# Strassen product (2,2) ahead of (5,1) in three feed-forward phases, with tiles 2 and 3 transposed half a product later, one copy in two halves, a bank of its own for a third row, and one evacuation moved to VectorE

## The chip, the cores and the metric

One core of a Trainium2 chip runs the kernel. The metric is device time in microseconds (us); the time given for a kernel is the median of several runs. The core has engines with a queue each, which take their instructions strictly in order: TensorE (PE) multiplies and transposes, VectorE (DVE) and ScalarE (ACT) work elementwise, GpSimd (POOL) and SyncE (SP) here mostly issue transfers. Engines wait for each other through semaphores. PE writes to eight banks of 128 x 512 floats; the operands come from on-chip memory, which the transfers fill.

## The reference, cut to what matters

The input is 512 positions of 1024 channels in float32. Two layers run, each as feed-forward, mixer, feed-forward, with a layer norm behind every one:

```python
def swiglu(x, w_gu, w_down):
    g, u = jnp.split(x @ w_gu, 2, axis=-1)
    return (jax.nn.silu(g) * u) @ w_down
...
for i in range(DEPTH):                      # DEPTH = 2
    x = layer_norm(ALPHA * x + 0.5 * swiglu(x, w_gu[i, 0], w_down[i, 0]), ln_g[i, 0], ln_b[i, 0])
    y = moba_attention(...) if i == 0 else pool_mixer(...)
    x = layer_norm(ALPHA * x + y, ln_g[i, 1], ln_b[i, 1])
    x = layer_norm(ALPHA * x + 0.5 * swiglu(x, w_gu[i, 1], w_down[i, 1]), ln_g[i, 2], ln_b[i, 2])
```

The width of the feed-forward is 2816. The order of the six phases, numbered n = 0 to 5, is: feed-forward, attention, feed-forward, feed-forward, pooling mixer, feed-forward.

## The kernel before, in words

**Matrix products.** The multiplications of the feed-forwards are done by Strassen's scheme: instead of eight products of quarter matrices there are seven (phase 0 takes one group in eight). A product (i, jj) is number i of group jj; a group makes 512 features of the gate and the up projection. Product 1 takes the first quarters, 2 the second, 5, 6 and 7 take sums and differences of quarters, 3 and 4 the rest. Every float32 operand is split into a rounded part `hi` and the remainder `lo`, and three matmuls (L110 to L112: lo x, hi x, hi x) stand for one. So a product is 24 matmuls of 128 x 512, and a "half product" (`q` 0 and 1 in `products`) 12. Each half takes one weight pair (`hi`, `lo`).

**What sets the order.** PE's order is that of the program (the engine is scheduled by hand); `order(eight)` lists the products of a feed-forward. The other engines' instructions are put in order by a scheduler, ahead of the run, which looks at when operands should be ready; each engine then keeps that fixed order. Tile pools give out buffers in turn, and a buffer's next writer waits for its last reader.

**Weights.** `pieces` is the list of loads, in order; `load` puts a piece of 512 KB on SP's queue (L302) and, where a sum of two quarters is wanted, has POOL's queue add the second in a transfer that accumulates (L304). `Quad` holds the pieces of one group: `p11`, `p12`, `s1` (a21 plus a22, an accumulation), `s3`, `p22`. With `apart` (groups 1 and 2 of phases 2, 3 and 5) DVE adds `s1` to `p11` for product 6 and `p11` to `p12` for product 3, at L158. `units` lists the weights in the order of use; `prepare` splits each into `hi` (ACT, L105) and `lo` (DVE, L106); the "lean" weights of the first products get their `lo` from ACT and an accumulating transfer on POOL's queue instead (L338). `p.uses` counts how many units still need a piece before its buffer may be loaded over.

**Start of a feed-forward.** The phase before ends with the normalisation of four tiles of 128 positions (`normalize`, L529 to L545: aggregate, variance, square root on ACT, reciprocal, one correction step, then the tile's two halves). `to_feature_major` transposes a normalised tile on PE (L487, eight transposes of 128 x 128), and ACT (L495) or DVE (L493) evacuates it into `st`, four pieces per half; the set `VEC` names the halves that DVE takes: tile 3, half 1. Tiles 0 and 1 are transposed inside the last products of the phase before. The transposes of tiles 2 and 3 are kept back in `late`, and `head` calls them after the two halves of product (1,1). From `st` the operands `x_1`, `x_2`, `x_3`, `x_5`, `x_6`, `x_7`, `x_4` are formed on DVE (differences, L429) and split (L105, L106).

**Behind a product.** `keep` copies the accumulator of products 1, 5 and 6 to on-chip memory (ACT, L735, one copy of 128 x 1024); products 2, 3, 4 and 7 finish a block: DVE adds the kept part (L745), ACT takes silu of one half (L727), DVE multiplies it by the other (L728), giving `gated`. Finished blocks wait in a list, and `to_features`, after products 5 and 4, transposes each on PE (L758, four transposes into one bank) and ACT copies it to `hT` (L759). The banks for it take turns: `TURNED` + 0 or 1, banks 6 and 7. With three blocks in the list the third uses the bank of the first again. `sums_at` gives the bank pair of product 1, 0 or 4; products 2 and 5 begin in pair `SECOND`, banks 2 and 3.

**Order around the change.** In phases 2, 3 and 5 the products start (1,1), (2,1), (1,2), (5,1), (6,1), (7,1), (3,1), (4,1) and go on with group 2: (2,2), (6,2), (5,2), and so on. (1,2) and (2,2) belong to group 2, whose weights are `w_gq[l, m, 2]` and `w_gq[l, m, 3]`, five quarters each.

Of the kernel before, what the change touches and what calls it, by code (L numbers as in the profile page):

```python
# [27 lines left out]
AF = mybir.ActivationFunctionType  # L28
# [34 lines left out]
VEC = ((3, 1),)  # L63
# [20 lines left out]
def trunk(ctx, tc, x_in, xt, rel_bias, ln_g, ln_b, w_gu, w_gq, w_dq, w_dh, w_v, a_in, a_out, b_in, b_group, b_scale, b_out, onehot, out):  # L84
    nc = tc.nc
# [11 lines left out]
    def bank(i, name):  # L97
        return banks8[:, i]

    def bank_pair(i):  # L100
        return banks8[:, i:i + 2]
# [20 lines left out]
    pieces, units, loaded, behind = [], [], [], {}  # L122

    def plain(src, lean=False):
        p = Piece(src)
        units.append((lambda: p.tile, (p,), src if lean else None))
# [51 lines left out]


    def order(eight):  # L180
        o = [(1, 1), (2, 1)] + ([(6, 1), (5, 1)] if eight else [(1, 2), (5, 1), (6, 1)])
        o += [(7, 1), (3, 1)] + [(1, 2)] * eight + [(4, 1)]
        steps = STEPS[not eight]
        for jj, following in zip(steps[1:], steps[2:] + (None,)):
            seven = [(i, jj) for i in (2, 6, 5, 7, 3, 4)]
            after = [(1, following)] if following is not None else []
            if jj == MIDDLE:
                group = [(i, FF) for i in LATER]
                o += seven[:-1] + group[:1] + seven[-1:] + group[1:] + after
            else:  # L190
                o += seven[:-1] + after + seven[-1:]
        return o + [(i, FF + 1) for i in DEEP]

    ORDERS = [order(True), order(False)]

    class Deep:
# [20 lines left out]
            units.append((lambda: p.tile, (p,)))  # L217

    BY_TRANSFER = ((1, 1), (2, 1), (1, 2))

    def in_turn(quads, kinds):
        pieces[-5 * len(quads):] = [q.pieces[k] for k in kinds for q in quads]
        return quads
# [14 lines left out]
    def two_quads(w, i):  # L238
        return in_turn([Quad(w[i + q]) for q in range(2)], (0, 2, 1, 3, 4))

    def ffn_units(l, m):
        eight = (l, m) == (0, 0)
        if eight:
            for i in FIRST:
                plain(w_gu[l, m, i])
        made = {}
        for i, jj in ORDERS[not eight]:
            lean = not eight and (i, jj) in BY_TRANSFER
            if (i, jj) == (1, 2) and not eight:
                for q in range(2):  # L250
                    plain(w_gq[l, m, 2 + q, 0], lean)
                b1 = pieces[-12:]
                pieces[-12:] = b1[0:2] + b1[4:6] + b1[2:4] + b1[10:] + b1[6:10]
                continue
            if jj not in made:
                if jj == 0:
                    made[jj] = [Quad(w_gu[l, m])]
                    pieces[-5:] = [made[jj][0].pieces[k] for k in (0, 2, 1, 3, 4)]
                elif jj == FF:
                    made[jj] = in_turn([Quad(w_dq[l, m, 0]), Quad(w_dq[l, m, 1]), narrow(Quad(w_dh[l, m]))], (0, 2, 1, 3, 4))  # L260
                elif jj == FF + 1:
                    made[jj] = in_turn([Deep(w_dq[l, m, q]) for q in (2, 3, 4)], range(5))
                else:
                    made[jj] = two_quads(w_gq[l, m], 2 * (jj - 1))
                for q in made[jj]:
                    if not eight and jj in (1, 2):
                        q.apart()
                    if i == 2:
                        q.p11.uses -= 1
            for q in made[jj]:  # L270
                q.unit(i, lean)

# [83 lines left out]
    def weights():  # L356
        taken[0] += 1
        while len(parts) < taken[0]:
            load_needed()
            prepare()  # L360
        return parts[taken[0] - 1]
# [7 lines left out]
    ax = glob.tile([P, NT, D], F32, name="ax")  # L369
# [110 lines left out]
            half, h = {1: (0, 0), 2: (1, 0), 3: (1, 1)}[i]  # L480
            return self.at(4 * half + k, (2 * h + t) * P, (2 * h + t + 1) * P)

    def to_feature_major(dest, t, half, xn, n, b):

        tp = bank(b + half, f"tp{t}_{half}")
        for i in range(4):
            nc.tensor.transpose(tp[:, i * P:(i + 1) * P], xn[:, (4 * half + i) * P:(4 * half + i + 1) * P], ident)  # L487
        src = dest.stage(half, t // 2)[:, :, (t % 2) * P:(t % 2 + 1) * P]
        for i in range(4):
            c, k = slice(i * P, (i + 1) * P), n * NK + 4 * half + i  # L490
            g, b = cols[:, k:k + 1], cols[:, NL + k:NL + k + 1]
            if (t, half) in VEC:
                nc.vector.tensor_scalar(src[:, i, :], tp[:, c], g, b, op0=ALU.mult, op1=ALU.add)  # L493
            else:
                nc.scalar.activation(src[:, i, :], tp[:, c], AF.Identity, scale=g, bias=b)  # L495
        dest.put(t, half, src)
# [52 lines left out]
    late = []  # L549
    residual = []  # L550
    row = [None]
# [137 lines left out]
    BANKS = {1: 0, 6: 0, 7: 0, 4: 0, 2: 1, 5: 1, 3: 1}  # L689
# [5 lines left out]
    SECOND, TURNED = 2, 6  # L695
# [3 lines left out]
    def ffn(n, x, dest):  # L699
        with tc.tile_pool(name=f"ffn{n}", bufs=1) as fp:  # L700
            hT = [fp.tile([P, GROUP, S], F32, name=f"hT{n}")]
            later, kept, waiting, turn = {}, {}, [], [0]
            eight, last = n == 0, n == len(lns) - 1
            sums_at = SUMS[not eight]
            x.lean = not eight

            def banks(b, count, name):
                return [bank((b + 4 * eight) % 8 + t, f"{name}_{t}") for t in range(count)]
# [23 lines left out]

            def keep(i, jj, acc):
                kept[i, jj] = fp.tile([P, 2, S], F32, tag=f"kept{BANKS[i]}", bufs=2 - BANKS[i], name=f"kept{n}_{jj}_{i}")
                nc.scalar.activation(kept[i, jj], acc, AF.Copy)  # L735

            def finish(i, jj, acc):

# [10 lines left out]

            def to_features(i, kept_back=1):  # L750

                while i in (5, 4) and len(waiting) > (i == 4) * kept_back:
                    out, f, h = waiting.pop(0)
                    turn[0] += 1
                    tp = banks(TURNED + turn[0] % 2, 1, f"ft{n}_{f}_{h}")[0].rearrange("p (c s) -> p c s", c=2)
                    for c in range(2):
                        for t in range(2):
                            nc.tensor.transpose(tp[:, c, t * P:(t + 1) * P], out[:, t, c * P:(c + 1) * P], ident)  # L758
                    nc.scalar.activation(features(f, 2)[:, :, h * 256:(h + 1) * 256], tp, AF.Copy)  # L759
# [172 lines left out]
            accs = {}  # L932
# [4 lines left out]
            def products(i, jj, b, amid=lambda q: None, outer=3, count=2):  # L937

                if i in (1, 2, 5):
                    accs[jj, BANKS[i]] = bank_pair(((SECOND if i != 1 else sums_at[jj]) + 4 * eight) % 8)  # L940
                acc = accs[jj, BANKS[i]]

                def one(w, k0, ts, first, last):
                    wh, wl = w
                    ks = wh.shape[-1] // 512
                    for k in range(ks):
                        c = slice(k * 512, (k + 1) * 512)
                        for t in ts:
                            mm3(acc[:, t], *b(k0 + k, t), wh[:, c], wl[:, c], first and k == 0 and i in (1, 2, 5),
                                last and k == ks - 1 and i in (2, 3, 4), True)  # L950

                for q in range(min(outer, count)):
                    one(weights(), 2 * q, range(2), q == 0, q == count - 1)
                    amid(q)
                ws = [weights() for q in range(outer, count)]
                for t in range(2):
                    for q, w in enumerate(ws, outer):
                        one(w, 2 * q, (t,), q == 0, q == count - 1)
                        amid((q, t))
                return acc  # L960

            def head(i, jj):

                def amid(q):
                    if i == 1:
                        late.pop(0)()
                    if (i, q) == (1, 1):
                        while len(parts) < taken[0] + 2:
                            load_needed()
                            prepare()  # L970
                        with tc.issue_after(x.last.ins):
                            next(sums)
                return amid
# [25 lines left out]
            def normalized(t):  # L999
                ins = norms[t].normalize(*params)  # L1000
                if not last:
                    b = {0: 0, 1: 2 if eight else 6, 2: 6, 3: 4}[t]
                    late.append(lambda: [to_feature_major(dest, t, half, ax[:, t, :], n, b) for half in range(2)])
                    residual.append((t, n))

            def down_second(i):
# [40 lines left out]
            for i, jj in ORDERS[not eight]:  # L1047
# [14 lines left out]
                if n == 0 and (i, jj) in RESIDUAL:  # L1062
                    with tc.issue_after(queued["load"].ins):
                        t = RESIDUAL.index((i, jj))
# [10 lines left out]
                if not eight and (i, jj) in ((1, 1), (2, 1)):  # L1075
                    acc = products(i, jj, of_x(x.parts[i]), head(i, jj))
                else:
                    acc = products(i, jj, of_x(x.parts[i]))
# [363 lines left out]
```

## Time and profile before

| | us |
|---|---|
| median of 3 runs | 1663.02 (1662.52 to 1663.35) |
| the profiled execution | 1662.03 |
| its span, first to last instruction | 1660.3 |
| PE busy | 1638.3 |
| DVE busy | 1359.5 |
| ACT busy | 957.2 |

The TensorE clock granted over the profiled execution was 0.998 of full speed. The profile is one execution; times in it are counted from the span's start. In a row of its timeline stand the start, the duration, the engine, the line of the kernel, the operation, the output and the inputs by their names (buffer numbers left out), the shapes, and in square brackets the idle time of the engine just before and who ended it. In a row of waits stand the engine and line that waited, who released it, the total of idle time, how often, and the longest. A row of transfers gives the issuing queue, the count, the size of each and the time from issue to landing. Phase 2 begins at about 545 us, phase 3 at about 885, phase 5 at about 1320.

### The profile page before, as it was taken

To read this page: it belongs to the slowest core of one execution; us is meant where nothing else is said; L and a number is where in the kernel's file an instruction comes from. 1 tells how busy PE (TensorE), PEld (TensorE's weight loads), DVE (VectorE), ACT (ScalarE), POOL (GpSimd) and SP (SyncE) were. 2 spreads that over 40 slices of the span, in tenths; PEclk is the share of its full clock that TensorE was granted. 3 is DMA by queue.
4 is the path that set the end of the run, shared out by engine and by line. 5 is a ranking of instruction groups with operands and counts; after the bars stand their busy time and mean duration, and the time that the engine had idled before them with its cause. 6 is when DMAs were issued, how large, how long until landed. Compare 5 with 4: busy or idle time off the path is not lost.

```text
span 1660.3 us, 21596 instructions
## 1 busy us (share of the span) xinstructions
PE 1638.3 (99%) x8051; PEld 1383.0 (83%) x8051; DVE 1359.5 (82%) x1707; ACT 957.2 (58%) x1288; POOL 175.0 (11%) x224
## 2 busy tenths in 40 slices
PE   9999999999999999999999999999999999999997
PEld 8888888898888878988887789888898878888886
DVE  7768898988675887888897878888987697779899
ACT  5555556666445755555667555556554665555562
POOL 1101101000001011101111111011000201110110
PEclk9999999999999999999999999999999999999999
DMA  9678688825157488757888886578734878866882
GB/s 303 188 221 243 155 231 216 247 57 177 54 151 189 115 243 214 199 142 214 227 224 204 242 220 187 146 213 229 219 114 128 196 199 216 242 152 174 222 214 76
DMA packets 99913, 315.62 MB, mean 190 GB/s; under 512 B 10144, under 2 KB 23496, under 8 KB 99808
## 3 DMA queue, kind: packets, MB, share of 16 engines
q1 hardware_dynamic: 71904, 214.99, 37.5%
q0 software_dynamic: 27904, 99.26, 32.6%
q8 instruction: 63, 1.03, 0.3%
q14 instruction: 42, 0.34, 0.1%
HBM read 312.09 MB, written 4.74 MB: 191 GB/s over the span
## 4 chain that ended last, share of the span: by engine, by line
PE 93%; DVE 3%; ACT 3%; issue 0%; DMA 0%; SPq 0%; DVEq 0%; ACTq 0%
PE banks L110 30%; PE banks L112 30%; PE banks L111 30%; PE banks L758 2%; ACT st L495 1%; PE banks L487 1%; DVE x L106 1%; DVE lo L106 1%; DVE st L429 1%; ACT hi L105 0%; ACT kept L735 0%; PE banks L1191 0%; ACT x L105 0%; DMA raw<-in_ffn_w_gu 0%; DVE ax L533 0%
## 5 line engine op out<-in xcount | busy, mean ns | idle before, releaser
L105 ACT ACTIVATE hi<-raw 128x1024 fp32r<-128x1024 f32 (+1 forms) x478 | 500.5, 1057 | 341.7 <-DVE lo L106 119.0
L106 DVE TENSOR_TENSOR lo<-raw,hi 128x1024 fp32r<-128x1024 f32 (+1 forms) x478 | 576.0, 1216 | 134.1 <-ACT hi L105 86.4
L110 PE MATMUL banks<-lo,x 128*128 128x512 f32 x1144 | 448.9, 392 | 4.3 <-ACT kept L735 3.4
L112 PE MATMUL banks<-hi,x 128*128 128x512 f32 x1144 | 445.8, 390 | 0.0
L111 PE MATMUL banks<-hi,x 128*128 128x512 f32 x1144 | 445.4, 389 | 0.0
L110 PEld LDWEIGHTS banks<-lo,x 128*128 128x128 f32 x1144 | 214.9, 188 | 50.6 <-ACT kept L735 4.7
L112 PEld LDWEIGHTS banks<-hi,x 128*128 128x128 f32 x1144 | 214.7, 188 | 45.0
L111 PEld LDWEIGHTS banks<-hi,x 128*128 128x128 f32 x1144 | 214.9, 188 | 43.1
L110 PE MATMUL banks<-lo,h 128*128 128x512 f32 x436 | 171.4, 393 | 0.0
L112 PE MATMUL banks<-hi,h 128*128 128x512 f32 x436 | 169.8, 389 | 0.0
L111 PE MATMUL banks<-hi,h 128*128 128x512 f32 x436 | 169.7, 389 | 0.0
L112 PE MATMUL banks<-x,lo 128*128 128x256 f32 (+1 forms) x488 | 152.0, 311 | 0.8 <-DVE lo L106 0.8
L110 PE MATMUL banks<-x,hi 128*128 128x256 f32 (+1 forms) x488 | 152.6, 313 | 0.0
L111 PE MATMUL banks<-x,hi 128*128 128x256 f32 (+1 forms) x488 | 151.7, 311 | 0.0
L304 POOL DMA_DIRECT2D raw<-in_ffn_w_gq x80 | 70.6, 893 | 655.1 <-DMA raw<-in_ffn_w_gq 164.4
L152 DVE TENSOR_TENSOR raw<-raw,raw 128x1024 f32<-128x1024 f32 (+1 forms) x86 | 102.6, 1193 | 24.0 <-DMA raw<-in_ffn_w_gq 14.2
L112 PEld LDWEIGHTS banks<-x,lo 128*128 128x128 f32 x488 | 93.0, 191 | 6.3 <-DVE lo L106 1.2
L110 PEld LDWEIGHTS banks<-x,hi 128*128 128x128 f32 x488 | 93.0, 191 | 5.6 <-DVE oT L106 0.2
L111 PEld LDWEIGHTS banks<-x,hi 128*128 128x128 f32 x488 | 93.0, 191 | 5.3
L112 PEld LDWEIGHTS banks<-hi,h 128*128 128x128 f32 x436 | 81.8, 188 | 17.1
L111 PEld LDWEIGHTS banks<-hi,h 128*128 128x128 f32 x436 | 81.9, 188 | 16.4
L110 PEld LDWEIGHTS banks<-lo,h 128*128 128x128 f32 x436 | 81.9, 188 | 16.4
(229 smaller groups left out, 2248.5 us busy)
## 6 DMA issues: line engine op xcount, KB each, us to landing
raw<-in_ffn_w_gq SPq DMA_DIRECT2D x206, 512.0 KB, 5.0
raw<-in_ffn_w_dq SPq DMA_DIRECT2D x100, 512.0 KB, 5.0
raw<-in_ffn_w_gq POOLq DMA_DIRECT2D x80, 512.0 KB, 7.5
raw<-in_ffn_w_dq POOLq DMA_DIRECT2D x52, 512.0 KB, 7.6
ax<-in_ln_b POOLq DMA_DIRECT2D x20, 512.0 KB, 8.2
raw<-in_ffn_w_gu SPq DMA_DIRECT2D x18, 512.0 KB, 5.2
raw<-in_a_w_in SPq DMA_DIRECT2D x16, 512.0 KB, 4.2
raw<-in_ffn_w_dh SPq DMA_DIRECT2D x20, 256.0 KB, 2.9
```

The costliest lines, as they stand in the source:

```text
L105: nc.scalar.activation(hi, src, AF.Copy)
L106: return nc.vector.tensor_tensor(lo, src, hi.bitcast(F32), op=ALU.subtract)
L110: nc.tensor.matmul(acc, sh, ml, start=first, stop=False, skip_group_check=shared)
L111: nc.tensor.matmul(acc, sh, mh, start=False, stop=False, skip_group_check=shared)
L112: nc.tensor.matmul(acc, sl, mh, start=False, stop=last, skip_group_check=shared)
L152: nc.vector.tensor_tensor(d, d, more, op=ALU.add)
L304: queued["acc"] = nc.gpsimd.dma_start(p.tile, p.plus, accum_op=ALU.add)
L429: nc.vector.scalar_tensor_tensor(out, a, scale, b, op0=ALU.mult, op1=op)
L487: nc.tensor.transpose(tp[:, i * P:(i + 1) * P], xn[:, (4 * half + i) * P:(4 * half + i + 1) * P], ident)
L495: nc.scalar.activation(src[:, i, :], tp[:, c], AF.Identity, scale=g, bias=b)
L758: nc.tensor.transpose(tp[:, c, t * P:(t + 1) * P], out[:, t, c * P:(c + 1) * P], ident)
```

## The change

In phases 2, 3 and 5 product (2,2) now follows (1,2), so that the start reads (1,1), (2,1), (1,2), (2,2), (5,1), (6,1), and it accumulates in banks 6 and 7. Its weight is the plain second quarter, loaded for itself as that of (1,2) already was (two loads more per phase on SP's queue, six in all). Tile 2 is transposed after the second half of (1,1) and tile 3 after the first half of (2,1), each half a product later than before. `keep` copies product (6,1) in two halves. In `to_features` a third row takes the bank pair of the next product 1 instead of the turning banks. DVE takes the evacuation of tile 1, half 1, too, where a feed-forward hands over to the next phase.

```diff
--- before.py
+++ after.py
@@ -178,11 +178,11 @@
 
 
     def order(eight):
-        o = [(1, 1), (2, 1)] + ([(6, 1), (5, 1)] if eight else [(1, 2), (5, 1), (6, 1)])
+        o = [(1, 1), (2, 1)] + ([(6, 1), (5, 1)] if eight else [(1, 2), (2, 2), (5, 1), (6, 1)])
         o += [(7, 1), (3, 1)] + [(1, 2)] * eight + [(4, 1)]
         steps = STEPS[not eight]
         for jj, following in zip(steps[1:], steps[2:] + (None,)):
-            seven = [(i, jj) for i in (2, 6, 5, 7, 3, 4)]
+            seven = [(i, jj) for i in (2, 6, 5, 7, 3, 4)][not eight and jj == 2:]
             after = [(1, following)] if following is not None else []
             if jj == MIDDLE:
                 group = [(i, FF) for i in LATER]
@@ -217,6 +217,7 @@
             units.append((lambda: p.tile, (p,)))
 
     BY_TRANSFER = ((1, 1), (2, 1), (1, 2))
+    HEAD = ((1, 2), (2, 2))
 
     def in_turn(quads, kinds):
         pieces[-5 * len(quads):] = [q.pieces[k] for k in kinds for q in quads]
@@ -246,11 +247,12 @@
         made = {}
         for i, jj in ORDERS[not eight]:
             lean = not eight and (i, jj) in BY_TRANSFER
-            if (i, jj) == (1, 2) and not eight:
+            if (i, jj) in HEAD and not eight:
                 for q in range(2):
-                    plain(w_gq[l, m, 2 + q, 0], lean)
-                b1 = pieces[-12:]
-                pieces[-12:] = b1[0:2] + b1[4:6] + b1[2:4] + b1[10:] + b1[6:10]
+                    plain(w_gq[l, m, 2 + q, i - 1], lean)
+                if i == 2:
+                    b1 = pieces[-14:]
+                    pieces[-14:] = b1[0:2] + b1[4:6] + b1[2:4] + b1[10:] + b1[6:10]
                 continue
             if jj not in made:
                 if jj == 0:
@@ -267,6 +269,9 @@
                         q.apart()
                     if i == 2:
                         q.p11.uses -= 1
+                    if i == 6:
+                        q.p11.uses -= 1
+                        q.p12.uses -= 1
             for q in made[jj]:
                 q.unit(i, lean)
 
@@ -480,7 +485,7 @@
             half, h = {1: (0, 0), 2: (1, 0), 3: (1, 1)}[i]
             return self.at(4 * half + k, (2 * h + t) * P, (2 * h + t + 1) * P)
 
-    def to_feature_major(dest, t, half, xn, n, b):
+    def to_feature_major(dest, t, half, xn, n, b, vec=VEC):
 
         tp = bank(b + half, f"tp{t}_{half}")
         for i in range(4):
@@ -489,7 +494,7 @@
         for i in range(4):
             c, k = slice(i * P, (i + 1) * P), n * NK + 4 * half + i
             g, b = cols[:, k:k + 1], cols[:, NL + k:NL + k + 1]
-            if (t, half) in VEC:
+            if (t, half) in vec:
                 nc.vector.tensor_scalar(src[:, i, :], tp[:, c], g, b, op0=ALU.mult, op1=ALU.add)
             else:
                 nc.scalar.activation(src[:, i, :], tp[:, c], AF.Identity, scale=g, bias=b)
@@ -732,7 +737,8 @@
 
             def keep(i, jj, acc):
                 kept[i, jj] = fp.tile([P, 2, S], F32, tag=f"kept{BANKS[i]}", bufs=2 - BANKS[i], name=f"kept{n}_{jj}_{i}")
-                nc.scalar.activation(kept[i, jj], acc, AF.Copy)
+                for t in (slice(0, 1), slice(1, 2)) if (i, jj) == (6, 1) and not eight else (slice(0, 2),):
+                    nc.scalar.activation(kept[i, jj][:, t], acc[:, t], AF.Copy)
 
             def finish(i, jj, acc):
 
@@ -749,10 +755,12 @@
 
             def to_features(i, kept_back=1):
 
+                row = 0
                 while i in (5, 4) and len(waiting) > (i == 4) * kept_back:
                     out, f, h = waiting.pop(0)
-                    turn[0] += 1
-                    tp = banks(TURNED + turn[0] % 2, 1, f"ft{n}_{f}_{h}")[0].rearrange("p (c s) -> p c s", c=2)
+                    row += 1
+                    turn[0] += row < 3
+                    tp = banks(TURNED + turn[0] % 2 if row < 3 else sums_at[1], 1, f"ft{n}_{f}_{h}")[0].rearrange("p (c s) -> p c s", c=2)
                     for c in range(2):
                         for t in range(2):
                             nc.tensor.transpose(tp[:, c, t * P:(t + 1) * P], out[:, t, c * P:(c + 1) * P], ident)
@@ -937,7 +945,7 @@
             def products(i, jj, b, amid=lambda q: None, outer=3, count=2):
 
                 if i in (1, 2, 5):
-                    accs[jj, BANKS[i]] = bank_pair(((SECOND if i != 1 else sums_at[jj]) + 4 * eight) % 8)
+                    accs[jj, BANKS[i]] = bank_pair(((TURNED if (i, jj) == (2, 2) and not eight else SECOND if i != 1 else sums_at[jj]) + 4 * eight) % 8)
                 acc = accs[jj, BANKS[i]]
 
                 def one(w, k0, ts, first, last):
@@ -962,12 +970,12 @@
             def head(i, jj):
 
                 def amid(q):
-                    if i == 1:
+                    if (i, q) in ((1, 1), (2, 0)):
                         late.pop(0)()
-                    if (i, q) == (1, 1):
                         while len(parts) < taken[0] + 2:
                             load_needed()
                             prepare()
+                    if (i, q) == (2, 0):
                         with tc.issue_after(x.last.ins):
                             next(sums)
                 return amid
@@ -1000,7 +1008,7 @@
                 ins = norms[t].normalize(*params)
                 if not last:
                     b = {0: 0, 1: 2 if eight else 6, 2: 6, 3: 4}[t]
-                    late.append(lambda: [to_feature_major(dest, t, half, ax[:, t, :], n, b) for half in range(2)])
+                    late.append(lambda: [to_feature_major(dest, t, half, ax[:, t, :], n, b, ((1, 1),) + VEC) for half in range(2)])
                     residual.append((t, n))
 
             def down_second(i):
```

Because the operations on DVE and ACT are put in order by the scheduler, it also moves instructions that the diff doesn't name. The rows below are in program order, with the engine's line, operation, output and inputs; the lines after the change are 5 to 8 higher for the same code (the reciprocal is L535 before and L540 after). The first place is DVE at the end of phase 2: `sm2_0` and `sm2_1` are the small values (variance and so on) of tiles 0 and 1 in its layer norm, `st2_0` their statistics, `raw` the buffers of loaded weights. Before:

```order
L529 BN_AGGR sm2_0_7207<-st2_0_7206 128x2
L529 BN_AGGR sm2_1_7210<-st2_1_7209 128x2
L530 TENSOR_SCALAR sm2_0_7207<-sm2_0_7207 128x1
L530 TENSOR_SCALAR sm2_1_7210<-sm2_1_7210 128x1
L535 RECIPROCAL sm2_0_7207<-sm2_0_7207 128x1
L535 RECIPROCAL sm2_1_7210<-sm2_1_7210 128x1
L536 SCALAR_TENSOR_TENSOR sm2_0_7207<-sm2_0_7207 128x1
L536 SCALAR_TENSOR_TENSOR sm2_1_7210<-sm2_1_7210 128x1
L537 TENSOR_SCALAR sm2_0_7207<-sm2_0_7207 128x1
L537 TENSOR_SCALAR sm2_1_7210<-sm2_1_7210 128x1
```

After:

```order
L534 BN_AGGR sm2_0_7212<-st2_0_7211 128x2
L534 BN_AGGR sm2_1_7215<-st2_1_7214 128x2
L535 TENSOR_SCALAR sm2_0_7212<-sm2_0_7212 128x1
L535 TENSOR_SCALAR sm2_1_7215<-sm2_1_7215 128x1
L158 TENSOR_TENSOR raw208_7160<-raw208_7160,raw212_7253 128x1024
L540 RECIPROCAL sm2_0_7212<-sm2_0_7212 128x1
L540 RECIPROCAL sm2_1_7215<-sm2_1_7215 128x1
L541 SCALAR_TENSOR_TENSOR sm2_0_7212<-sm2_0_7212 128x1
L541 SCALAR_TENSOR_TENSOR sm2_1_7215<-sm2_1_7215 128x1
L542 TENSOR_SCALAR sm2_0_7212<-sm2_0_7212 128x1
L542 TENSOR_SCALAR sm2_1_7215<-sm2_1_7215 128x1
```

The sum of two weight pieces that product (6,1) of phase 3 needs (L158) stands between the variance and the reciprocal of tiles 0 and 1; it stood some 50 rows further back before, between splits of weights. `raw208` comes from SP's queue, and the last write to `raw212` is an accumulation on POOL's queue.

The second place is DVE at the end of phase 4, where the last output weights have been split and tile 0's residual is added from a bank (L519 before, L524 after) and its statistics are taken. Before:

```order
L106 TENSOR_TENSOR lo408_10878<-raw308_10517,hi408_10877 128x1024
L106 TENSOR_TENSOR lo409_10890<-raw309_10523,hi409_10889 128x1024
L519 SCALAR_TENSOR_TENSOR ax_75<-banks8_74,ax_75 128x512
L523 BN_STATS st4_0_10919<-ax_75 128x6
L519 SCALAR_TENSOR_TENSOR ax_75<-banks8_74,ax_75 128x512
L523 BN_STATS st4_0_10919<-ax_75 128x6
```

After:

```order
L106 TENSOR_TENSOR lo408_10888<-raw312_10527,hi408_10887 128x1024
L106 TENSOR_TENSOR lo409_10900<-raw313_10533,hi409_10899 128x1024
L158 TENSOR_TENSOR raw315_10710<-raw315_10710,raw319_10842 128x1024
L524 SCALAR_TENSOR_TENSOR ax_75<-banks8_74,ax_75 128x512
L528 BN_STATS st4_0_10928<-ax_75 128x6
L524 SCALAR_TENSOR_TENSOR ax_75<-banks8_74,ax_75 128x512
L528 BN_STATS st4_0_10928<-ax_75 128x6
```

Here the same sum of phase 5 (`raw315` plus `raw319`, again an accumulation on POOL's queue) stands in front of tile 0's first add.

The third place is DVE at the start of phase 2, from the gate of (2,1) on; the names give phase, group and product, so `gated2_1_2` is the gate of (2,1) and `gated2_2_2` that of (2,2). Before:

```order
L728 SCALAR_TENSOR_TENSOR gated2_1_2_4887<-kept2_1_1_4861,gated2_1_2_4887 128x512
L158 TENSOR_TENSOR raw118_4297<-raw118_4297,raw122_4532 128x1024
L106 TENSOR_TENSOR x2_6_4892<-st2_4690,x2_6_4892 128x1024
L106 TENSOR_TENSOR lo161_4915<-raw123_4535,hi161_4914 128x1024
L106 TENSOR_TENSOR lo162_4920<-raw118_4297,hi162_4919 128x1024
L158 TENSOR_TENSOR raw119_4303<-raw119_4303,raw123_4535 128x1024
L429 SCALAR_TENSOR_TENSOR st2_4690<-st2_4690 128x1024
L158 TENSOR_TENSOR raw120_4309<-raw120_4309,raw118_4297 128x1024
```

After:

```order
L733 SCALAR_TENSOR_TENSOR gated2_1_2_4891<-kept2_1_1_4838,gated2_1_2_4891 128x512
L434 SCALAR_TENSOR_TENSOR st2_4689<-st2_4689 128x1024
L106 TENSOR_TENSOR lo161_4917<-raw127_4899,hi161_4916 128x1024
L106 TENSOR_TENSOR lo162_4923<-raw122_4532,hi162_4922 128x1024
L106 TENSOR_TENSOR x2_6_4896<-st2_4689,x2_6_4896 128x1024
L106 TENSOR_TENSOR lo163_4953<-raw123_4535,hi163_4952 128x1024
L158 TENSOR_TENSOR raw118_4297<-raw118_4297,raw122_4532 128x1024
L434 SCALAR_TENSOR_TENSOR st2_4689<-st2_4689 128x1024
L751 TENSOR_TENSOR kept2_2_1_4950<-kept2_2_1_4950,banks8_74 128x1024
L106 TENSOR_TENSOR lo164_4958<-raw118_4297,hi164_4957 128x1024
L106 TENSOR_TENSOR x2_7_4964<-st2_4689,x2_7_4964 128x1024
L733 SCALAR_TENSOR_TENSOR gated2_2_2_4991<-kept2_2_1_4950,gated2_2_2_4991 128x512
```

The gate of (2,2) is now eleven rows behind that of (2,1), with the splits of the weights of (2,2), (5,1) and (6,1) and the operands 6 and 7 between them; it was 37 rows behind before. On PE its transposes follow those of (2,1) directly, at the end of (5,1).

## The prediction

> **What bounds the kernel now.** I read the busy shares first, then PE's waits, then PE's rows one by one, and last the other engines and the transfers where the change moves work.
>
> ```profile
> PE 1638.3 (99%) x8051; PEld 1383.0 (83%) x8051; DVE 1359.5 (82%) x1707; ACT 957.2 (58%) x1288; POOL 175.0 (11%) x224
> 874.65 0.39 PE L111 MATMUL banks<-hi,h_7b 128*128 128x512 f32 x1
> 874.88 0.39 PE L112 MATMUL banks<-hi,h_7b 128*128 128x512 f32 x1
> 875.11 1.03 PE L487 MATMUL banks<-ident,ax 128*128 128x128 f32 x8
> ```
>
> PE is busy for 99% of the span and its order is fixed by hand, so the time is PE's work plus the moments at which it waits. The work does not change: the number of products and transposes is the same. Matmuls start 0.23 us apart (874.65 to 874.88), so 24 of them, one product, take 5.45 us and half a product 2.72. A row is 0.39 us long, so an idle time counted from a row's end leaves out 0.16 us of each wait. The waits, with total, count and longest, are these four rows:
>
> ```profile
> PE banks L758 <- ACT hT L759: 3.6, 3, 1.2
> PE banks L110 <- ACT kept L735: 3.4, 3, 1.2
> PE banks L487 <- DVE ax L545: 1.6, 1, 1.6
> PE banks L110 <- DVE lo L106: 0.9, 2, 0.4
> ```
>
> That is 9.5 us in nine waits, 10.9 with 0.16 us added to each: all that the change aims at, and 0.65% of the span. Since PE has so little idle time, any new wait of several microseconds in front of a PE instruction goes into the time whole. So what decides is whether DVE, which is in order and 82% busy, now meets a wait that it did not have.
>
> **The waits that are mended.** (a) L758 on hT: three rows of transposes stood in line for two turning banks. Now no more than two rows stand together: the three waits go, 3.6 + 3 x 0.16 = 4.1 us saved. (b) kept: PE waits for one copy of 128x1024.
>
> ```profile
> 583.74 1.02 ACT L735 ACTIVATE kept<-banks 128x1024 f32<-128x1024 f32 x1 [0.49 <-PE banks L112]
> 580.77 0.58 ACT L759 ACTIVATE hT<-banks 128x512 f32<-128x512 f32 x1
> ```
>
> A copy of half the width is near 0.58 us (the second row), and the first half's last matmul ends three matmuls, 0.68 us, ahead of the product's end, so the first copy is almost over when PE arrives. I leave 0.3 us per wait (bounds 0 and 0.7): 3.4 + 0.5 - 0.9 = 3.0 saved. (c) L487 on ax, in phase 3: tile 2 is transposed 2.72 us later and its wait is 1.6 + 0.16, so it goes: 1.8 saved. What is late next there is nothing, as long as its DVE chain starts on time. (d) lo: DVE, not the transfer, sets it; the weights of (2,2) are now the ones that are made last before their use, and I leave 0.4 us twice: 0.4 saved. Sum 9.3 us.
>
> **What the reordering adds at the head.** The gate of (2,2) used to be due a whole group of products later. Now its transposes follow (5,1), right behind those of (2,1).
>
> ```profile
> L106 DVE TENSOR_TENSOR lo<-raw,hi 128x1024 fp32r<-128x1024 f32 x13 | 15.5, 1217 | 0.0
> 577.61 0.60 PE L758 MATMUL banks<-ident,gated 128*128 128x128 f32 x4
> 563.71 1.22 DVE L429 SCALAR_TENSOR_TENSOR st<-st 128x1024 f32<-128x1024 f32 x1
> 573.48 2.35 DVE L106 TENSOR_TENSOR lo<-raw,hi 128x1024 fp32r<-128x1024 f32 x2
> 570.60 0.69 DVE L728 SCALAR_TENSOR_TENSOR gated<-kept,gated 128x512 f32<-128x512 f32 x1
> 571.21 1.22 DVE L158 TENSOR_TENSOR raw<-raw,raw 128x1024 f32<-128x1024 f32 x1
> ```
>
> Operations of 128x1024 on DVE follow each other every 1.135 us (two in 2.35, less the overlap of 0.08), a gate every 0.61 (570.60 to 571.21). Operand 5's difference, at 563.71 before, starts 2.72 us later with tile 3, so about 566.5; from it to the gate of (2,2) DVE has fourteen operations of 128x1024 and two gates: 14 x 1.135 + 1.22 = 17.1, ready at 583.6 to 584.1. The transposes of (2,2) are due one product after 577.61, less the lo wait of 0.6, plus 0.3 for the row ahead of them: 582.8 or so. So PE waits 1.0 us (bounds 0 and 1.5) in each of the three phases 2, 3 and 5: 3.0 us lost. Two more loads of 512 KB per phase lie on SP's queue ahead of later ones; their first uses have several microseconds to spare, so I cost them at nothing; without that cover each would cost up to the 3 us that a load takes. One evacuation moved from ACT to DVE makes DVE normalise tiles 2 and 3 of phases 0 and 3 in pairs, later than before:
>
> ```profile
> 340.67 1.00 DVE L545 TENSOR_SCALAR ax<-ax,sm 128x512 f32<-128x512 f32 x2
> 342.29 1.04 PE L487 MATMUL banks<-ident,ax 128*128 128x128 f32 x8
> ```
>
> Tile 2's first half left DVE 1.1 us before its transposes; two statistics and the chain of the other tile in front of it take some 1.5, so 0.4 us lost, twice (bounds 0 and 0.8 each): 0.8 lost. Up to here the change gains 9.3 - 3.0 - 0.8 = 5.5 us.
>
> **Two weight sums in new places.** This is the term that decides. A sum of two loaded pieces (L158) stood deep in the head of phases 3 and 5, after everything urgent. In the changed order one stands on DVE between the variance and the reciprocal of tiles 0 and 1 at the end of phase 2, and one in front of tile 0's residual at the end of phase 4. Each reads a piece that POOL's queue accumulates.
>
> ```profile
> 866.61 1.47 POOL L304 DMA_DIRECT2D raw<-in_ffn_w_gq  x1
> raw<-in_ffn_w_gq POOLq DMA_DIRECT2D x1, 512.0 KB, 15.8
> DMA  2696699999999999999999999999999999999999
> 870.56 0.27 DVE L530 TENSOR_SCALAR sm<-sm 128x1 f32<-128x1 f32 x2
> 871.54 0.26 DVE L535 RECIPROCAL sm<-sm 128x1 f32<-128x1 f32 x2 [0.71 <-ACT sm L531]
> 872.39 1.91 DVE L545 TENSOR_SCALAR ax<-ax,sm 128x512 f32<-128x512 f32 x4
> ```
>
> The transfer behind the first sum is issued at 866.61 and takes 15.8 us, to 882.4: from 862 to 890 the transfer engines are full (the third row, 0.7 us a digit), and two weights and an accumulation are ahead of it in its queue. The loads and the queue ahead of it do not change, so I take the same landing. DVE then adds (1.22) and goes on from the reciprocal: 883.6, and 872.39 - 871.54 + 0.54 = 1.39 to the first normalised half of tile 0, 885.0. PE wants it at 875.11 (the transposes shown above), and nothing behind them on PE may pass. That is **9.9 us lost**; tile 1 follows in time. Behind the sum DVE has only what PE itself waits for, so nothing else piles up.
>
> ```profile
> 1294.24 0.87 POOL L304 DMA_DIRECT2D raw<-in_ffn_w_gq  x1 [1.87 <-PE banks L110]
> raw<-in_ffn_w_gq POOLq DMA_DIRECT2D x1, 512.0 KB, 15.0
> 1300.16 0.69 DVE L519 SCALAR_TENSOR_TENSOR ax<-banks,ax 128x512 f32<-128x512 f32 x1 [2.21 <-PE banks L112]
> 1302.88 0.69 DVE L519 SCALAR_TENSOR_TENSOR ax<-banks,ax 128x512 f32<-128x512 f32 x1 [1.30 <-PE banks L112]
> 1305.84 1.00 DVE L545 TENSOR_SCALAR ax<-ax,sm 128x512 f32<-128x512 f32 x2
> 1306.76 0.69 DVE L519 SCALAR_TENSOR_TENSOR ax<-banks,ax 128x512 f32<-128x512 f32 x1
> 1311.28 1.00 DVE L545 TENSOR_SCALAR ax<-ax,sm 128x512 f32<-128x512 f32 x2
> 1310.85 1.03 PE L487 MATMUL banks<-ident,ax 128*128 128x128 f32 x8
> 1314.46 1.03 PE L487 MATMUL banks<-ident,ax 128*128 128x128 f32 x8
> 1323.52 1.03 PE L487 MATMUL banks<-ident,ax 128*128 128x128 f32 x8
> ```
>
> The second lands at 1294.24 + 15.0 = 1309.2; the sum ends at 1310.4. Tile 0 then needs an add and its statistics (1.46) and, from the second add to the first normalised half, 1305.84 + 0.54 - 1302.88 = 3.5: 1315.4. PE wants it at 1310.85, 4.5 us lost. Tile 1 is ready 1311.28 + 0.54 - 1306.76 = 5.1 after 1315.8, at 1320.9; PE comes to it 3.61 after tile 0's transposes, at 1319.0: 1.9 more. Tile 2, now half a product later than its 1323.52, has slack again. That is **6.4 us lost**. A third sum that moved, at the end of phase 1, has slack of over 10 us behind it and costs nothing.
>
> **Sum.** 9.9 + 6.4 - 5.5 = 10.8 us on the profiled execution's 1662.0, so 1672.8; the median of the runs is 1.0 above that execution, so I say 1673.8 us.
>
> **A rule of the skill against this.** The Trainium skill, in "DMA: Bandwidth & Descriptors", section "Anatomy of one DMA — SWDGE (gpsimd) path", gives a transfer from the GpSimd side 2.0 us plus its bytes over 436,000 per us, an estimate of 3.2 us for 512 KB. By it the first piece would be there at 869.8 and the second at 1297.4, both ahead of DVE, and the sums would cost nothing but their 1.2 us. The trace has 15.8 and 15.0 us for these two, since neither has the engines to itself; the forecast goes by those.
>
> **Rivals.** *The pieces are there in time.* The page's median for such an accumulation is below what these two took:
>
> ```profile
> raw<-in_ffn_w_gq POOLq DMA_DIRECT2D x80, 512.0 KB, 7.5
> DVE raw L152 <- DMA raw<-in_ffn_w_gq: 14.2, 6, 3.9
> ```
>
> Landing within 5 us of issue (871.5 and 1299) takes both losses away: faster, 1673.8 - 16.3 = 1657.5. Against it speak the two transfers' own times, with the same queue in front, and the second row: sums of the other kind do hold DVE for up to 3.9 us on such transfers. 7 in 100; half of this is the rule above. *The pieces come about 4 us earlier*, if the lighter queue of SP lets them: 16.3 - 8 leaves 8.3 - 5.5, so 1665.8. 13 in 100, for the margin is small against a chain of queued transfers. *The mends don't hold, or the late DVE carries on*: kept, hT and gates cost PE what they did, and the gain of 5.5 falls to 1.5: 1677.8. 10 in 100. The forecast has 70.
>
> **Range and chances.** From 1666.0, next to the second rival, to 1678.0, the third; the terms' bounds (up to 4 us for the mends, 1 to 2 for each landing) lie inside. What a measurement of this kernel can tell from no change is 0.2%, 3.3 us: slower from 1666.3 on. The forecast, the third rival and half of the second are slower: 86. The rest of the second is the same: 7. The first is faster: 7.
>
> **What would show it.** PE idle of near 10 us ahead of the transposes of tile 0 in phase 3, released by DVE's normalisation, with DVE idle before L158 on a transfer; another near 4.5 and one near 2 us at the start of phase 5. The waits of L758 on hT gone, those on kept under 0.5 each, three of about 1 us on the gate of (2,2). If DVE stands at L158 for less than 2 us at both places, the prediction is wrong and the kernel is faster.

## The result, and the profile after

The changed kernel takes 1675.0 us (median of 6 runs, 1673.05 to 1675.89) against 1662.68 us for the kernel before: 1.0073 times as long, with a 95% interval of 1.0061 to 1.0086. The forecast was 1673.8 us. The execution that was profiled took 1675.89 us, 13.9 more than the profiled one of before.

First the busy row of the page, and PE's waits of the changed kernel (engine and line that waited, who released it; total, times, longest, in us):

```profile
PE 1643.8 (98%) x8051; PEld 1385.9 (83%) x8051; DVE 1361.3 (81%) x1719; ACT 951.3 (57%) x1279; POOL 174.7 (10%) x224
PE banks L492 <- DVE ax L550: 14.3, 3, 9.5
PE banks L766 <- DVE gated L733: 2.2, 3, 0.8
```

The rows of before for hT, kept, lo and tile 2 of phase 3 have no successor: all nine waits that the change aimed at are gone, but for remnants of 0.17 to 0.24 us in five places (kept and lo), 0.9 us in all from start to start. In their place stand three on the gate of (2,2), and three on normalised tiles, of 9.5, 4.4 and 0.4 us. DVE's own rows at the two places show where those come from:

```profile
871.04 0.27 DVE L535 TENSOR_SCALAR sm<-sm 128x1 f32<-128x1 f32 x2
882.66 1.23 DVE L158 TENSOR_TENSOR raw<-raw,raw 128x1024 f32<-128x1024 f32 x1 [11.35 <-DMA raw<-in_ffn_w_gq]
883.80 0.22 DVE L540 RECIPROCAL sm<-sm 128x1 f32<-128x1 f32 x2
884.64 1.91 DVE L550 TENSOR_SCALAR ax<-ax,sm 128x512 f32<-128x512 f32 x4
...
1317.67 1.22 DVE L158 TENSOR_TENSOR raw<-raw,raw 128x1024 f32<-128x1024 f32 x1 [11.45 <-DMA raw<-in_ffn_w_gq]
1318.82 0.68 DVE L524 SCALAR_TENSOR_TENSOR ax<-banks,ax 128x512 f32<-128x512 f32 x1
1323.08 1.00 DVE L550 TENSOR_SCALAR ax<-ax,sm 128x512 f32<-128x512 f32 x2
```

DVE has nothing to do but to wait, 11.35 and 11.45 us, at a sum that no product needs yet, with the normalisation behind it. The two accumulations, each alone in a window of the view of transfers, took 15.5 us (issued at 867.09) and 15.6 us (at 1302.09). PE's rows for tile 0 and tile 1 of both places:

```profile
885.24 1.97 PE L492 MATMUL banks<-ident,ax 128*128 128x128 f32 x8 [9.55 <-DVE ax L550]
890.69 1.04 PE L492 MATMUL banks<-ident,ax 128*128 128x128 f32 x8
...
1323.68 1.97 PE L492 MATMUL banks<-ident,ax 128*128 128x128 f32 x8 [4.41 <-DVE ax L550]
1330.00 1.04 PE L492 MATMUL banks<-ident,ax 128*128 128x128 f32 x8
```

Counted from start to start, PE loses 9.70 us before 885.24 and 4.56 us before 1323.68. One thing is new: between tile 0 and tile 1 pass 5.45 and 6.32 us, where it was 3.62 and 3.61 before, for the same work, with no wait in between. The view by stretches of time (length, PE busy with its instructions, granted clock, share of the transfer engines, GB/s) shows why:

```profile
877.00:879.00 2.00, 0.00 (x0) 0.93 1.06 270
879.00:881.00 2.00, 0.00 (x0) 0.50 1.07 281
...
888.00:889.00 1.00, 1.00 (x4) 0.51 1.09 217
889.00:890.00 1.00, 1.00 (x6) 1.00 1.09 217
...
1322.00:1323.00 1.00, 0.00 (x0) 0.74 0.00 0
1328.00:1329.00 1.00, 1.00 (x4) 0.50 0.00 0
1329.00:1330.00 1.00, 1.00 (x5) 0.85 0.00 0
```

While PE idles its granted clock falls to one half, and it stays there for 3.7 and 5.6 us after PE has begun again (to 889.0 and 1329.3). That cost 1.8 and 2.7 us.

### The profile page after: what moved, and what is told of

It is laid out like the page before. It is cut to its first block, busy times and chain, and to the rows that moved or that the text cites. A ratio compares the mean times of both kernels' runs of the same rounds, so it can differ in the third digit from the quotient of the medians.

```text
span 1674.1 us, 21627 instructions
## 1 busy us (share of the span) xinstructions
PE 1643.8 (98%) x8051; PEld 1385.9 (83%) x8051; DVE 1361.3 (81%) x1719; ACT 951.3 (57%) x1279; POOL 174.7 (10%) x224
## 4 chain that ended last, share of the span: by engine, by line
PE 88%; DVE 6%; DMA 3%; ACT 2%; issue 1%; SPq 0%; DVEq 0%; ACTq 0%; POOLq 0%
PE banks L110 28%; PE banks L112 28%; PE banks L111 28%; DMA raw<-in_ffn_w_gq 2%; PE banks L766 2%; DVE lo L106 1%; DVE x L106 1%; PE banks L492 1%; DVE st L434 1%; ACT st L500 1%; PE banks L1199 0%; DMA raw<-in_ffn_w_gu 0%; DVE kept L751 0%; ACT x L105 0%; DVE st L498 0%
```

## The experiments

**Sums behind the operands.** The only change is where DVE may place what is prepared after (2,2):

```diff
+                elif not eight and (i, jj) == (2, 2):
+                    with tc.issue_after(x.last.ins):
+                        retire(2)
                 else:
                     retire(2)
```

> The changed kernel with one thing more: what is prepared after product (2,2) is queued behind the last split of an operand on DVE, so both weight sums (L158) stand again among the splits in the head of phases 3 and 5. If the two sums in front of the normalisation are the cause: the waits before the transposes of tile 0 (9.7 us in phase 3, 4.6 us in phase 5 in the changed kernel's trace) are gone, and with them some 4 us of slow matmuls behind them; left are 2.6 us for the gates of (2,2) and 0.5 us in phase 1, so 1656 us (1654.5 to 1658). If the new order itself or the six more loads are the cause, tile 0 or the next product waits for something else instead and the time stays at 1668 us or more. If only half of the loss hangs on them: about 1665 us.

1662.17 us, 1.0001 times before (0.9992 to 1.001). The waits on tile 0 and the slow matmuls behind them are gone, so the cause stands. But two kinds of waits are there that the changed kernel had not:

```profile
PE banks L110 <- DVE lo L106: 3.4, 3, 1.1
PE banks L766 <- DVE gated L733: 2.1, 3, 0.8
PE banks L110 <- ACT kept L741: 1.4, 3, 0.5
585.20 3.48 DVE L158 TENSOR_TENSOR raw<-raw,raw 128x1024 f32<-128x1024 f32 x3
589.88 0.50 PE L110 MATMUL banks<-lo,x 128*128 128x512 f32 x1 [1.15 <-DVE lo L106]
```

Behind the gate DVE now makes three sums in a row before the second weight of (6,1) is split, and PE waits for it. In the changed kernel that split follows the gate directly:

```profile
585.61 0.68 DVE L733 SCALAR_TENSOR_TENSOR gated<-kept,gated 128x512 f32<-128x512 f32 x1
586.22 1.22 DVE L106 TENSOR_TENSOR lo<-raw,hi 128x1024 fp32r<-128x1024 f32 x1
```

Counted from start to start the two kinds cost 3.9 and 1.9 us over the three phases. On ACT a split of 1.05 us had come between the two halves of the copy of (6,1); what put it there was not tried apart. So the early sum was also a gain: it took one operation of 1.1 us out of the stretch in which DVE is the bottleneck, and with it gone from there the two other sums stood behind those splits. All three expectations missed the time: the cause was right, its price without a good place for the sum was not.

**The same, and tile 1 evacuated by ACT again** (`vec` left at its default at the hand-over).

> As the run before, and tile 1, half 1, evacuated by ACT again at the three hand-overs. If the evacuation on DVE is a cost and no mend once tile 2 is transposed half a product later: the 0.5 us wait in phase 1 goes and nothing comes, 1655.5 us. If it was what mended the wait of 1.7 us on tile 2 in phase 3: that wait comes back in part, 1657 us or more.

1661.75 us against 1662.17, 0.9997 times before (0.9988 to 1.0006); the runs overlap (1660.94 to 1662.54 against 1661.7 to 1663.36). No wait on tile 2 came back. Both expectations counted from the 1656 us that the first run did not give, and the 0.5 us wait in phase 1 that one of them wanted to mend is not in the first run's trace either. Moving this evacuation brought no gain. In this pair and in the next one the version with ACT has the lower median, by 0.4 and 1.3 us with overlapping runs; whether the evacuation on DVE costs that much was not settled.

**The gate of (2,2) transposed later**, behind (4,1), with the sums as in the first run; and the same with tile 1 on ACT.

```diff
-                while i in (5, 4) and len(waiting) > (i == 4) * kept_back:
+                while i in (5, 4) and len(waiting) > (i == 4) * kept_back + hold:
...
-                to_features(i, 2 if not eight and jj == 1 else 1)
+                to_features(i, 2 if not eight and jj == 1 else 1, int(not eight and (i, jj) == (5, 1)))
```

> The changed kernel with the sums queued behind as in the first run, and the gate of (2,2) transposed after product (4,1) instead of (5,1), in phases 2, 3 and 5. If the three waits of 0.7 to 1.0 us on that gate are the price of the early place of (2,2) alone: they go and nothing comes, 2.6 us less than the first run, 1653.5 us (1652.5 to 1655). If what is late there is DVE as a whole: the next matmuls, of (6,1), wait for their weights instead, and it is within 1 us of the first run.

> Sums behind, gate of (2,2) later, and tile 1, half 1, on ACT: the version meant to beat both kernels. If the three effects add: 1653 us (1652 to 1654.5), 0.6% below the kernel before. If the evacuation on DVE is worth something: 1654.5 us or more.

1665.72 us and 1664.40 us, 1.0022 (1.0013 to 1.0031) and 1.0015 (1.0006 to 1.0024) times before: both slower. The waits on the gate are gone and those on lo have more than doubled:

```profile
PE banks L110 <- DVE lo L106: 7.4, 3, 2.6
1356.20 0.73 PE L110 MATMUL banks<-lo,x 128*128 128x512 f32 x1 [2.53 <-DVE lo L106]
1356.50:1359.50 3.00, 3.00 (x8) 0.50 0.73 188
```

PE comes to (6,1) earlier and waits there for DVE. The gate was only the first to show that DVE is late. The second expectation had this mechanism, but not its price, 3.5 us more than the first run: the waits on lo grew by 4.0 us and those on the gate, 2.6, went, and behind the last of the waits on lo the clock was halved again (the last row, from the view by stretches), which cost 1.9 us. The three sums still stood ahead of these splits; a later gate with the sums in a better place was not tried.

**The old order, with the rest of the change**: `order`, `HEAD`, the uses of the pieces and the bank pair as before.

> The changed kernel with the products in the old order ((2,2) behind (4,1), its weights loaded as before), and all else of the change kept: tiles 2 and 3 half a product later, the copy in two halves, the bank for a third row, the evacuation. The sums stand among the splits again by themselves. If the order is what moved the sums, and the mends work without it: no wait before tile 0, waits on kept, hT and tile 2 of phase 3 gone, about 1654 us (1652.5 to 1657). If the mends need the new order: the hT or kept waits are left and it is 1659 us or more.

1670.79 us, 1.0049 times before (1.0034 to 1.0064). No tile 0 waits, and no kept, hT or tile 2 either, so the mends work in the old order too. But neither theory gave the time, for this came:

```profile
PE banks L110 <- DVE lo L106: 11.0, 8, 3.0
597.76 1.22 DVE L158 TENSOR_TENSOR raw<-raw,raw 128x1024 f32<-128x1024 f32 x1 [3.02 <-DMA raw<-in_ffn_w_gq]
```

With tiles 2 and 3 half a product later and no product (2,2) to fill the time, DVE's splits are late at (6,1), (3,1) and (4,1); one stretch is again a sum that waits for its accumulation. From start to start these waits are 12.6 us, more than the 10.9 that the mends took away, and the longest two, of 3.0 and 2.9 us, halved the clock, which cost 1.6 us each. That the later tiles need the new order is the likely reading; the shares of the two were not taken apart.

**PE kept busy while it waits.** Transposes of the identity into tile 0's bank, overwritten by tile 0's own:

```diff
         tp = bank(b + half, f"tp{t}_{half}")
+        for _ in range({2: 84, 4: 38}.get(n, 0) if (t, half) == (0, 0) else 0):
+            nc.tensor.transpose(tp[:, 0:P], ident, ident)
```

> The changed kernel with transposes of the identity put on PE into the bank of tile 0 just before tile 0's own, 84 at the end of phase 2 and 38 at the end of phase 4 (some 9.1 and 4.1 us of work that is overwritten). In the changed kernel's trace the granted clock is 0.50 for about 3 us after the wait in phase 3 and for 4 to 5 us after that in phase 5, and matmuls start 0.43 us apart there instead of 0.23. If idleness of PE causes that: the clock stays at 1.0, the matmuls behind tile 0 start 0.23 us apart, 1.9 us come back in phase 3 and 2.9 us in phase 5, less the wait of up to 1.9 us on tile 1 in phase 5 that I had forecast and that the slow matmuls hid: 1675.0 - 3 = 1672 us (1670 to 1673.5). If it is not idleness (a transfer, or what PE runs): the slow matmuls stay and the time stays at 1675 us.

1671.9 us, 3.1 less than the changed kernel (1.0058 times before, 1.0041 to 1.0074). In the view by stretches the clock stays whole, through the filled wait and behind it, and tile 1 in phase 5 now waits:

```profile
873.00:883.40 10.40, 9.73 (x87) 1.00 1.05 276
883.40:886.00 2.60, 2.58 (x16) 1.00 1.07 233
1325.20:1328.00 2.80, 2.77 (x16) 1.00 0.00 0
1325.23 1.11 PE L494 MATMUL banks<-ident,ax 128*128 128x128 f32 x8 [1.34 <-DVE ax L552]
```

So the slow matmuls come from PE's idleness, and they had hidden a wait of 1.5 us from start to start, for which the forecast had 1.9.

**Fewer transfers in the queue.** `BY_TRANSFER` without (1,1): the weights of that product get their `lo` on DVE.

> The changed kernel with the lo weights of product (1,1) made on DVE, so that two transfers of 512 KB fewer stand in POOL's queue ahead of each of the two accumulations; the sums stay where they are, in front of the normalisation. If the place of the accumulation in its queue sets the loss: it lands some 7.5 us earlier, DVE waits under 4 us at the sum of phase 3 and under 2.5 us in phase 5, tile 0 loses under 2.5 us in phase 3 and nothing in phase 5, 1657 to 1662 us. If the sums' place as such or the order is the cause: 1672 us or more, plus four operations more on DVE per phase.

1671.13 us, 1.0053 times before (1.0038 to 1.0068), between the two expectations. DVE's rows at the two sums:

```profile
877.78 1.23 DVE L158 TENSOR_TENSOR raw<-raw,raw 128x1024 f32<-128x1024 f32 x1 [5.01 <-DMA raw<-in_ffn_w_gq]
...
1313.89 1.23 DVE L158 TENSOR_TENSOR raw<-raw,raw 128x1024 f32<-128x1024 f32 x1 [9.61 <-DMA raw<-in_ffn_w_gq]
```

In phase 3 the accumulation took 10.8 us instead of 15.5, DVE waited 5.0 us instead of 11.35, and PE lost 5.7 us before tile 0 instead of 9.7, with the sum still in front of the normalisation (two short rows further forward). In phase 5 little changed: there two other weights and a residual still stood ahead in the queue, the accumulation took 14.8 us, and PE lost 4.1 us instead of 4.6. So the expectation missed both: the gain in phase 3 was smaller than it said, in phase 5 there was next to none, and the clock was halved behind both waits as before. The loss follows the landing, as far as phase 3 shows it.

**A place for the sums.** Behind the normalisation of the last tile (`normed` notes it), no further; then operand 7 behind the gate of (2,2); then the sums behind tile 2 instead of tile 3. The diff is that of the second run; the first has no line with `next(sums)` and none of those around it, the third has `normed[n - 1, 2]`.

```diff
+                elif not eight and (i, jj) == (2, 2):
+                    with tc.issue_after(normed[n - 1, 3].ins):
+                        retire(2)
+                    with tc.issue_after(ins.ins):
+                        next(sums)
...
-                            if i != 2:
+                            if i == 6:
                                 next(sums)
```

> The changed kernel with what is prepared after product (2,2) queued on DVE behind the normalisation of tile 3, no further: the two sums stand right behind it, after their accumulations have landed and before the splits of the head. The first run showed that a sum put deep into the head costs 1.3 us at the second weight of (6,1) and 0.6 us at kept, three times, 5.8 us in all. If DVE's full head is the cause of that: both waits go, tile 0 waits for nothing, left are 2.6 us on the gates, 1656 us (1654.5 to 1658). If a sum anywhere behind tile 0 costs its 1.2 us of DVE later: the waits of the first run stay and it is 1660 us or more.

> As the run before, and operand 7's difference and split queued on DVE behind the gate of (2,2) instead of ahead of it. If the gate waits because of what stands ahead of it on DVE: it comes one to two operations of 1.14 us earlier, its three waits of 0.7 to 1.0 us go, nothing else comes, 1653.5 us (1652 to 1655). If the chain of the gate itself is what is late: 1656 us, or later when (7,1) waits for operand 7.

> As the run before, with the sums behind the normalisation of tile 2, ahead of tile 3's. If tile 3, now half a product later, has room for one operation of 1.2 us: the same time within 0.7 us. If not: a wait on tile 3 of up to 1 us at the start of phase 3 or 5, and 1654.5 us or more.

1655.53 us (0.9958 times before, 0.9944 to 0.9971), 1653.55 us (0.9945, 0.9932 to 0.9957) and 1652.99 us (0.9943, 0.9930 to 0.9955). All three came as the first theory of each had it. The first run's only waits in the feed-forwards' heads over 0.25 us are the three on the gate:

```profile
PE banks L769 <- DVE gated L736: 2.1, 3, 0.8
```

In the other two these are gone as well, with nothing in their place; the last two cannot be told apart. The last is the fastest version found, 22 us below the changed kernel. With the place of the sums alone mended the change is worth 0.4%, with operand 7 moved too 0.6%; as it was made it lost that, and 0.7% more, at two places of one instruction.

## Why the prediction was right

**The deciding term.** Two sums of loaded weights in front of the normalisation, each waiting for an accumulation in its queue: forecast 9.9 and 4.5 us before tile 0, measured 9.70 and 4.56. The transfers' times from the trace of before (15.8 and 15.0 us) held (15.5 and 15.6); the 3.2 us that the prediction worked out from the Trainium skill ("DMA: Bandwidth & Descriptors", section "Anatomy of one DMA — SWDGE (gpsimd) path") did not describe these two. The first run and the last three show that the place of the sums is the cause, the run with fewer transfers, in phase 3, that the landing sets the size. The row of the transfer engines that the prediction calls full from 862 us on is full from 865.5 on, still ahead of the issue at 866.6.

**The mends.** All nine waits went, the forecast left 0.9 us on kept and 0.8 us on lo, measured are 0.5 and 0.4. Here the forecast was right in part for a reason that it did not have: with the sums back in DVE's full head both kinds of wait return, in another place (5.8 us). The rival "pieces in time" said 1657.5; with a good place for the sums it was 1655.5.

**The gate of (2,2)**: three waits of 1.0 forecast, 0.96, 0.73 and 0.96 measured. The rival reading that the gate alone is late fell: it is DVE's row of work up to (6,1).

**Tile 2 at the end of phases 0 and 3** (the hand-over to a mixer): 0.4 us each forecast, 0.54 in the first, under 0.25 in the second.

**What was missing** is the slow restart, 1.8 and 2.7 us: the prediction let a wait of PE go into the time whole, and no more than whole. What was too much is tile 1 in phase 5, 1.9 us, which the slow restart covered. From the terms as measured, nine waits gone (10.9), their remnants 0.9, gates 2.6, tile 2 0.5, tile 0 14.3 and the restarts 4.5, the sum is 11.9 of the 13.9 us between the two profiled executions. Of the rest 1.3 us lies in the first 15 us, ahead of all changed code, in waits for the first weights that also differ among the other runs; the remainder is spread over excesses under 0.25 us and was not followed. So the mechanism and its size were right, and that the time came within 1.2 us of the forecast was luck in part: the restarts that it lacked and the wait on tile 1 that did not come pull in opposite directions, and between the profiled executions the forecast was 10.8 us where 13.9 were measured.

## What to carry to other kernels

An in-order engine that is near its limit turns any early instruction that waits for a transfer into a stop for all that stands behind it, so after a change of order look first at which of its waits on transfers moved ahead of urgent work, and take their landing from the trace, queue included, not from a transfer's time alone. The same operation can also be too late: between "before the normalisation" (12.3 us lost against before) and "deep in the head" (nothing gained) lay a place, behind the last normalised tile, that gained 7.0 us, and 9.0 with operand 7 moved as well. And when a wait is taken away, read who is late next: removing the wait on the gate by moving its consumer made the kernel slower (with the sums deep in the head), moving its competitors made it faster (with the sums ahead of the head).

## What the runs showed of the hardware

In the changed kernel PE's granted clock fell to 0.50 at 878.7 and 1322.5 us, 3.2 and 3.4 us after its last matmul was through (875.5 and 1319.1), and came back at 889.0 and 1329.3, 3.7 and 5.6 us after it had work again; matmuls of 128x512 started 0.43 us apart in between instead of 0.23. With transposes of no use in the wait it did not fall. In the kernel before, whose waits in the feed-forwards are 1.7 us at most, it was 0.998 over the whole and fell only behind PE's last instruction.

Waits between these lengths can do it too. With the gate transposed later the clock fell in phase 5 with a wait of 2.5 us, but not with those of 2.6 and 2.3 us in phases 2 and 3; in the old order it fell with two waits of 3.0 and 2.9 us, the second time 1.6 us after PE had begun again. In all these traces the spells at half clock that end with PE at work last 3.4, 6.8 or 10.2 us (10.2 and 6.8 in the changed kernel), which is one, two or three times 3.4. So whether a wait of some 2.5 us costs more than itself depends on more than its length.

The Trainium skill describes this in "TensorE: Matmul & The Clock Gate", section "Part 1: The HAM clock gate (the "warmup" mystery)": half the clock after an idle window of about 3.4 us, the full clock after about as long of sustained work, in windows that run freely. The lengths of the spells agree with such windows; the waits of 2.5 to 3.0 us that halved the clock are shorter than one, and there the measurement decides.
